# A feed-forward block's input products as 7 products in place of 8, in 2 x 2 blocks

## The chip, the cores and the metric

One Trainium2 chip; the program runs on one of its cores. The metric is the device time of one execution in microseconds (us). TensorE (PE) multiplies, VectorE (DVE), ScalarE (ACT) and GpSimd (POOL) work on tiles in SBUF and PSUM, SyncE (SP) issues the transfers from HBM.

## What is computed

One layer of a streaming encoder over 560 tokens (16 meta tokens, 512 frames of a new stream, 32 of a running one): a feed-forward block with its norm, a mixer (retention and latent attention), a norm, and a second feed-forward block with a norm. All in float32. The part that matters here:

```python
def swiglu(x, w_in, w_out):
    g, u = jnp.split(x @ w_in, 2, axis=-1)          # w_in 1024 x 5632
    return (jax.nn.silu(g) * u) @ w_out             # w_out 2816 x 1024

def ffn_block(x, w_in, w_out, g, b):
    return layer_norm(DN_ALPHA * x + 0.5 * swiglu(x, w_in, w_out), g, b)
...
h = ffn_block(h, ffn1_w_in, ffn1_w_out, ln1_g, ln1_b)
mix = jnp.concatenate([ret_y, mla_y], -1) @ w_mix_out
h = layer_norm(DN_ALPHA * h + mix, ln2_g, ln2_b)
return ffn_block(h, ffn2_w_in, ffn2_w_out, ln3_g, ln3_b)
```

## The kernel before

Activations lie with features on partitions: `xs[hf][k]` is row tile k (128 of the 1024 features) of token half hf, as a pair of a rounded part and the rest. Halves are 288 and 272 tokens in FFN 1 and the first norm, 272 and 272 from the mixer's output on, where the meta tokens are dropped. Products carry float32 in three matmuls (`mm3`): rounded weights by rounded and by remaining activations, remaining weights by rounded activations. Weights come from HBM in tiles of 128 x 1024 (`load_w`): ACT rounds one (`wh`, L155), DVE subtracts for the rest in two pieces of 512 (`wl`, L157).

A feed-forward block (`ffn`) takes 22 column pairs j, one tile of the gate's weights and one of the up weights. For each and for each half, 2 x 8 row tiles x 3 matmuls, then `glu`: ACT silu of the gate (L395), DVE times up (L396), ACT rounds `h` (L168), DVE takes the rest (L169). So a pair is 96 matmuls, and a block 2112 for its input products. The first two pairs are done row tile by row tile, half 0 and then half 1, since weights and inputs land then (FFN 1) or half 1 is still in its norm (FFN 2). After all pairs comes the output product over 22 inner tiles: row tiles m = 0 to 5 for both halves, then 6 and 7 of half 0, then 6 and 7 of half 1, so that half 0's norm runs beside half 1's products.

`LayerNorm` takes each finished row tile (`add`: residual from its pair in two DVE operations, L283 and L284, or an addition, L286), centres all 8 tiles when two are there (`centre`, L305, and `prep`, L275 and L276), sums up moments on POOL, the last on DVE (L319), and `finish` has PE sum them over the partitions, takes the root on DVE and scales.

The order on PE is what the class `Weave` emits: among tasks whose data should be there by an estimated clock, the one of highest priority goes on. On the other engines a scheduler sets the order, each engine goes through its list in turn, and an instruction that waits holds up those behind it. Pools limit what can be ahead: 3 raw weight tiles `wr`, 4 rounded `wh` and `wl`, 12 half tiles, 8 PSUM banks.

## Time and profile before

| | |
|---|---|
| runs | 1149.88, 1150.14, 1151.75 us (median 1150.14) |
| span of the profiled execution | 1151.2 us |
| PE busy | 1124.9 us, 98% |
| DVE, ACT, POOL busy | 558.9, 370.8, 150.6 us |
| PE's mean granted clock | 0.981 |

The times come from runs without the profiler, the rows of the trace from one profiled execution of 1151.2 us; its times are counted from the start of its span. FFN 1 fills about the first 400 us, the mixer the next 330, FFN 2 the rest.

### The profile page before, as it was taken

What the parts mean: (1) busy time and instruction counts of PE and PEld (TensorE: products, weight loads), DVE (VectorE), ACT (ScalarE), POOL (GpSimd) and SP (SyncE); (2) the same over time, 40 slices, a digit from 0 to 9 for tenths busy, and PEclk for the clock granted to TensorE, in tenths of its full rate; (3) what the DMA queues carried; (4) which work ended last, traced back from release to release, by engine and by line L of the source; (5) the groups of instructions that cost most, each with busy time, mean ns of one, the idle gap of its engine ahead of it and who ended that gap; (6) DMA issues with size and microseconds to landing.
All of it is one profiled execution on the core that took longest, in us unless ns stands there. A gap on an engine that the chain in (4) does not pass through costs nothing.

```text
span 1151.2 us, 20255 instructions
## 1 busy us (share of the span) xinstructions
PE 1124.9 (98%) x8505; PEld 1085.4 (94%) x8505; DVE 558.9 (49%) x1225; ACT 370.8 (32%) x709; POOL 150.6 (13%) x169
## 2 busy tenths in 40 slices
...
GB/s 235 100 102 74 83 101 74 83 96 74 87 88 88 137 181 70 30 91 42 38 42 38 60 115 23 53 96 89 89 95 75 95 90 82 94 83 88 83 133 78
DMA packets 34458, 99.90 MB, mean 87 GB/s; under 512 B 4352, under 2 KB 9856, under 8 KB 34368
## 3 DMA queue, kind: packets, MB, share of 16 engines
...
q14 instruction: 24, 0.20, 0.1%
...
## 4 chain that ended last, share of the span: by engine, by line
PE 87%; DVE 7%; issue 2%; ACT 2%; POOL 0%; DMA 0%; SPq 0%; DVEq 0%; POOLq 0%; ACTq 0%
PE ps L130 79%; PE sc L130 2%; PE ax L130 2%; DVE wl L157 1%; DVE y L366 1%; DVE lnd L319 1%; PE ro L130 1%; PE ex L130 1%; DMA w<-in_w1f 0%; ACT y L377 0%; DVE y L275 0%; PE sc L134 0%; PE kv L130 0%; ACT x L168 0%; DVE y L305 0%
## 5 line engine op out<-in xcount | busy, mean ns | idle before, releaser
L130 PE MATMUL ps<-x,wh 128*128 128x272 f32 (+1 forms) x3456 | 674.1, 293 | 0.8 <-POOL x L169 0.4
L130 PEld LDWEIGHTS ps<-x,wh 128*128 128x128 f32 x3456 | 553.0, 191 | 8.6 <-issue 4.9
L130 PE MATMUL ps<-x,wl 128*128 128x272 f32 (+1 forms) x1728 | 504.7, 292 | 0.0
L157 DVE TENSOR_TENSOR wl<-wr,wh 128x512 fp32r<-128x512 f32 (+1 forms) x340 | 237.8, 727 | 242.7 <-ACT wh L155 242.2
L130 PEld LDWEIGHTS ps<-x,wl 128*128 128x128 f32 x1728 | 329.9, 191 | 0.0
L155 ACT CAST wh<-wr 128x1024 fp32r<-128x1024 f32 (+1 forms) x170 | 173.4, 1021 | 345.1 <-PE ps L130 236.2
L130 PE MATMUL ps<-h,wh 128*128 128x272 f32 (+1 forms) x1408 | 269.7, 290 | 0.0
L130 PEld LDWEIGHTS ps<-h,wh 128*128 128x128 f32 x1408 | 222.3, 188 | 0.3
L130 PE MATMUL ps<-h,wl 128*128 128x272 f32 (+1 forms) x704 | 204.1, 290 | 0.0
L130 PEld LDWEIGHTS ps<-h,wl 128*128 128x128 f32 x704 | 132.6, 188 | 0.0
L396 DVE TENSOR_TENSOR sil<-sil,ps 128x272 f32<-128x272 f32 (+1 forms) x88 | 38.8, 441 | 181.1 <-PE ps L130 170.8
L319 POOL TENSOR_TENSOR lnd<-y,y 128x272 f32<-128x272 f32 (+1 forms) x4 | 11.3, 2820 | 592.1 <-DVE y L305 296.8
L168 ACT CAST h<-sil 128x272 fp32r<-128x272 f32 (+1 forms) x88 | 36.6, 419 | 129.9 <-DVE sil L396 129.9
L395 ACT ACTIVATE sil<-ps 128x272 f32<-128x272 f32 (+1 forms) x88 | 35.0, 397 | 78.3 <-PE ps L130 78.2
L169 DVE TENSOR_TENSOR h<-sil,h 128x272 fp32r<-128x272 f32 (+1 forms) x88 | 38.9, 443 | 21.9 <-ACT h L168 21.9
L312 ACT ACTIVATE y<-y 128x272 f32<-128x272 f32 (+1 forms) x48 | 20.0, 432 | 54.8 <-DVE y L286 43.8
L355 POOL TENSOR_TENSOR y<-y,lnmb 128x272 f32<-128x272 f32 (+1 forms) x30 | 26.3, 906 | 39.3 <-ACT lnmb L346 24.6
L319 POOL TENSOR_TENSOR lnd<-lnd,y 128x272 f32<-128x272 f32 (+1 forms) x20 | 18.7, 933 | 90.6 <-DVE y L286 90.5
L319 POOL TENSOR_TENSOR lnq<-lnq,y 128x272 f32<-128x272 f32 (+1 forms) x30 | 28.9, 964 | 8.6 <-ACT y L312 7.4
L467 DVE TENSOR_TENSOR rope<-ps,rt 64x272 f32<-64x272 f32 (+3 forms) x28 | 12.4, 444 | 29.8 <-PE ps L130 29.2
L130 PE MATMUL ps<-mix,wh 128*128 128x272 f32 x128 | 24.9, 291 | 0.0
L130 PE MATMUL ps<-mix,ww 128*128 128x272 f32 x192 | 24.4, 286 | 0.0
...
## 6 DMA issues: line engine op xcount, KB each, us to landing
wr<-in_w SPq DMA_DIRECT2D x84, 512.0 KB, 3.6
wr<-in_w1o SPq DMA_DIRECT2D x20, 512.0 KB, 3.5
wr<-in_wmix SPq DMA_DIRECT2D x20, 512.0 KB, 3.5
wr<-in_w2o SPq DMA_DIRECT2D x20, 512.0 KB, 3.5
wr<-in_wmo SPq DMA_DIRECT2D x8, 512.0 KB, 3.7
...
```

Of the source, the lines that this page charges most:

```text
L130: nc.tensor.matmul(out, lhsT, rhs, start=start, stop=stop)
L155: nc.scalar.copy(hi[:, :nb * P], raw[:, :nb * P])
L157: nc.vector.tensor_tensor(out=lo[:, c], in0=raw[:, c], in1=f32(hi[:, c]), op=ALU.subtract)
L168: nc.scalar.copy(x[:, 0, cs], src)
L169: (eng or nc.vector).tensor_tensor(out=x[:, 1, cs], in0=src, in1=f32(x[:, 0, cs]), op=ALU.subtract)
L312: nc.scalar.activation(self.lo(m), self.hi(m), AF.Square)
L319: e.tensor_tensor(out=acc, in0=part(0) if first else acc, in1=part(m), op=ALU.add)
L355: nc.gpsimd.tensor_tensor(out=self.hi(m), in0=self.hi(m), in1=mb, op=ALU.subtract)
L366: (nc.gpsimd if self.sink and self.wide and m > 5 else nc.vector).tensor_tensor(out=self.hi(m), in0=self.hi(m), in1=r, op=ALU.mult)
L395: nc.scalar.activation(s, pg[:, :n], AF.Silu)
L396: nc.vector.tensor_tensor(s, s, pu[:, :n], ALU.mult)
L467: nc.vector.tensor_tensor(t[lo_], src_ps[hi_], sin[hi_, cs], ALU.mult)
```

## The change

The input products of a column pair go by blocks: A is the pair's weights, gate and up by two halves of four row tiles (a11, a12 of the gate, a21, a22 of up), B the activations, the same halves of row tiles by two halves of tokens (b11, b21 of half 0, b12, b22 of half 1). Of Strassen's scheme in Winograd's form seven products of 4 row tiles are taken for eight: a11 b11, a12 b21, s2 t2, s1 t1, s3 t3, s4 b22, a22 t4. The sums s of weights are made for each pair by POOL (`quads`), the sums t of activations once for a block by DVE and POOL (`sums`), and the seven results are added up on DVE (`rest`). Pair 0 is done as before; pairs 1 and 2 take their first two products in half 0's part of the start (`early`). Token halves are equal now, 280 and 280 in FFN 1, by putting 8 of the 16 meta tokens at the end (`wrap` copies them back in the mixer). Low parts of `h` go from DVE to POOL. The residual is kept whole (`xr`). The output product comes in three parts, after 8, 8 and 6 pairs, each added into the residual; in the last, m = 0 and 1 go for both halves, then 2 to 7 of half 0, then of half 1. Weights are rounded in pieces of 512 on ACT too. The estimated time of a matmul in `Weave` is longer.

```diff
-NBIG = 63
+NBIG = 45
...
+NPART = 26
+NRAW = 4
...
 NA = 288
-NB = T - NA
+HB = T // 2
+HM = NM // 2
+TW = T + HM
 HQ = TQ // 2
+KQ = KD // 2
+NFIRST = 4
+GROUPS = (8, 8, 6)
 
...
-    def mm(out, lhsT, rhs, start, stop):
+    def mm(out, lhsT, rhs, start, stop, more=False):
         n = rhs.shape[-1]
-        nc.tensor.matmul(out, lhsT, rhs, start=start, stop=stop)
-        wv.t += max(25.0, n / 2.4 + 2.5) if rhs.dtype == F32R else max(58.0, n / 0.6 + 5.0)
+        nc.tensor.matmul(out, lhsT, rhs, start=start, stop=stop, skip_group_check=more)
+        wv.t += max(110.0, n / 2.4 + 11.7) if rhs.dtype == F32R else max(98.0, n / 0.6 + 8.0)
 
...
+    def load_raw(src, nb):
+        raw = wp.tile([P, 8 * P], F32, tag="wr", name=nm("wr"))
         nc.sync.dma_start(raw[:, :nb * P], src)
...
+        return raw
...
+    def rounded(src, n=4 * P, early=False):
+        hi, lo = [tp.tile([P, 2 * NA], F32R, tag="big", name=nm(s)) if early else part(F32R, s) for s in ("wh", "wl")]
+        nc.scalar.copy(hi[:, :n], src)
+        nc.vector.tensor_tensor(out=lo[:, :n], in0=src, in1=f32(hi[:, :n]), op=ALU.subtract)
+        return hi, lo
...
+    xr = [[xp_.tile([P, NA], F32, tag="xr", name=nm("xr")) for _ in range(KD)] for _ in range(2)]
...
     for k in range(KD):
...
-        tc.keep_in_program_order(nc.sync.dma_start(t, xa[k]))
+        tc.keep_in_program_order(nc.sync.dma_start(xr[0][k][:, :HB], xa[k]))
...
-        split(xs[0][k], slice(0, NA), t, nc.gpsimd if k % 2 else nc.vector)
-        nc.scalar.copy(first_h[q][:, c], raw)
-        nc.vector.tensor_tensor(first_l[q][:, c], raw, f32(first_h[q][:, c]), ALU.subtract)
+        split(xs[0][k], slice(0, HB), xr[0][k][:, :HB], nc.gpsimd if k % 2 else nc.vector)
+        first.append(rounded(raw, early=True))
...
-        t = half(s="xin")
-        last_in = tc.keep_in_program_order(nc.sync.dma_start(t[:, :NB], xb[k]))
+        last_in = tc.keep_in_program_order(nc.sync.dma_start(xr[1][k][:, :HB], xb[k]))
...
-        split(xs[1][k], slice(0, NB), t[:, :NB], nc.gpsimd)
+        split(xs[1][k], slice(0, HB), xr[1][k][:, :HB], nc.vector if k % 2 else nc.gpsimd)
...
+        def part(self, m, ps):
+            if self.scaled[m]:
+                nc.vector.tensor_tensor(self.hi(m), self.hi(m), ps[:, :self.n], ALU.add)
+            else:
+                nc.vector.scalar_tensor_tensor(self.hi(m), self.hi(m), self.scale, ps[:, :self.n], ALU.mult, ALU.add)
+            self.scaled[m] = True
...
-            if self.y[m] is None:
-                self.y[m] = tp.tile([P, 2, NA], F32, tag="big", name=nm("y"))
-                xh, xl = f32(self.xt[m][:, 0, self.cs]), f32(self.xt[m][:, 1, self.cs])
-                nc.vector.scalar_tensor_tensor(self.hi(m), xl, self.scale, ps[:, :n], ALU.mult, ALU.add)
-                nc.vector.scalar_tensor_tensor(self.hi(m), xh, self.scale, self.hi(m), ALU.mult, ALU.add)
-            else:
-                nc.vector.tensor_tensor(self.hi(m), self.hi(m), ps[:, :n], ALU.add)
+            self.part(m, ps)
...
             for m in range(8):
-                if self.y[m] is None:
-                    self.prep(m)
+                if self.scaled[m]:
+                    nc.vector.tensor_tensor(self.hi(m), self.hi(m), self.c, ALU.subtract)
                 else:
-                    nc.vector.tensor_tensor(self.hi(m), self.hi(m), self.c, ALU.subtract)
+                    nc.vector.scalar_tensor_tensor(self.hi(m), self.hi(m), self.scale, self.c, ALU.mult, ALU.subtract)
+                    self.scaled[m] = True
...
+    def quads(j, wi, e=(nc.gpsimd, nc.gpsimd)):
+        g, u = load_raw(wi(2 * j), KD), load_raw(wi(2 * j + 1), KD)
+        a11, a12, a21, a22 = g[:, :4 * P], g[:, 4 * P:], u[:, :4 * P], u[:, 4 * P:]
+        s1, s2, s4 = part(s="s1"), part(s="s2"), part(s="s4")
+        e[0].tensor_tensor(out=s1, in0=a21, in1=a22, op=ALU.add)
+        e[0].tensor_tensor(out=s2, in0=s1, in1=a11, op=ALU.subtract)
+        e[1].tensor_tensor(out=a21, in0=a11, in1=a21, op=ALU.subtract)
+        e[1].tensor_tensor(out=s4, in0=a12, in1=s2, op=ALU.subtract)
+        return a11, a12, {"s1": s1, "s2": s2, "s3": a21, "s4": s4, "a22": a22}
+    def ffn(first, wi, wo, cs, lns, ready=(None, None)):
+        n = cs[0].stop - cs[0].start
+        s_ = slice(0, n)
...
+        ts = {}
...
+        def sums():
+            for b in range(KQ):
+                b11, b21, b12, b22 = col(xr, b, 0), col(xr, b + KQ, 0), col(xr, b, 1), col(xr, b + KQ, 1)
+                t1, t2, t3, t4 = [half(n, "ts") for _ in range(4)]
+                for t, x, y, e in ((t1, b12, b11, nc.vector), (t2, b22, t1, nc.vector), (t3, b22, b12, nc.gpsimd),
+                                   (t4, b21, t2, nc.gpsimd)):
+                    e.tensor_tensor(out=t, in0=x, in1=y, op=ALU.subtract)
+                for name, t, e in (("t2", t2, nc.vector), ("t1", t1, nc.vector), ("t3", t3, nc.vector), ("t4", t4, nc.gpsimd)):
+                    ts[name, b] = pair("ts")
+                    split(ts[name, b], s_, t, e)
...
+        def product(ps, w, name, start=True):
+            for b in range(KQ):
+                c = slice(b * P, b * P + P)
+                mm3(ps[:, :n], lambda _: (w[0][:, c], w[1][:, c]), 0, right(name, b), s_, start and b == 0, b == KQ - 1, not start)
+        def keep(hf, j, sil, up):
+            nc.vector.tensor_tensor(sil, sil, up, ALU.mult)
             h[hf][j] = pair("h")
-            split(h[hf][j], slice(0, n), s)
...
+            split(h[hf][j], s_, sil, nc.gpsimd)
+        def silu(ps):
+            t = half(n, "sil")
+            nc.scalar.activation(t, ps, AF.Silu)
+            return t
+        def rest(j, t1, sil0, p2, f):
+            w = {i: rounded(f[i]) for i in ("s2", "s1", "s3", "s4")}
+            pb = bank()
+            product(pb, w["s2"], "t2")
+            nc.vector.tensor_tensor(t1, t1, pb[:, :n], ALU.add)
+            yield 0
+            pc = bank()
+            product(pc, w["s1"], "t1")
+            y5 = half(n, "y5")
+            nc.vector.tensor_tensor(y5, t1, pc[:, :n], ALU.add)
+            yield 0
+            pd = bank()
+            product(pd, w["s3"], "t3")
+            c22 = half(n, "c22")
+            nc.vector.tensor_tensor(c22, y5, pd[:, :n], ALU.add)
+            yield 0
+            pe = bank()
+            product(pe, w["s4"], "b22")
+            nc.vector.tensor_tensor(y5, y5, pe[:, :n], ALU.add)
+            nc.scalar.activation(y5, y5, AF.Silu)
+            keep(1, j, y5, c22)
+            yield 0
...
+            if sil0 is None:
+                sil0 = p2()
+                yield 0
+            product(pd, rounded(f["a22"]), "t4", False)
+            nc.vector.tensor_tensor(t1, t1, pd[:, :n], ALU.add)
+            keep(0, j, sil0, t1)
+            yield 0
...
+        def early():
...
+            for k in range(KD):
+                for u in range(4):
+                    w, b = first(k, u)
+                    mm3(ps[u][:, :n], w, b, xs[0][k], s_, k == 0, k == KD - 1 or u > 1 and k == KQ - 1, u > 1 and k >= KQ)
+                yield 0
+                if k == KQ - 1:
+                    for u in (2, 3):
+                        t1[u - 1] = big(NA, "t1")[:, :n]
+                        nc.scalar.copy(t1[u - 1], ps[u][:, :n])
+            sil0 = {u - 1: silu(ps[u][:, :n]) for u in (2, 3)}
+            sil = silu(ps[0][:, :n])
+            keep(0, 0, sil, ps[1][:, :n])
+            if ready[1]:
+                yield ready[1]
+            f = {1: quads(1, wi, (nc.gpsimd, nc.vector))[2]}
+            sums()
+            ps = [bank() for _ in range(2)]
+            for k in range(KD):
+                for u in range(2):
+                    w, b = first(k, u)
+                    mm3(ps[u][:, :n], w, b, xs[1][k], s_, k == 0, k == KD - 1)
+                yield 0
+            sil = silu(ps[0][:, :n])
+            keep(1, 0, sil, ps[1][:, :n])
+            f[2] = quads(2, wi, (nc.gpsimd, nc.vector))[2]
+            for j in (1, 2):
+                yield from rest(j, t1[j], sil0[j], None, f[j])
...
+        def column(j):
+            a11, a12, f = quads(j, wi)
+            pa = bank()
+            product(pa, rounded(a11), "b11")
+            t1 = half(n, "t1")
+            nc.scalar.copy(t1, pa[:, :n])
+            yield 0
+            w2 = rounded(a12)
+            def p2():
+                product(pa, w2, "b21", False)
+                return silu(pa[:, :n])
+            yield from rest(j, t1, None, p2, f)
...
+        def out(k0, nk, last):
+            def load(m):
+                return load_w(wo[m, :, k0 * P:(k0 + nk) * P], nk)
+            def products(ps, w, hf):
+                for k in range(nk):
+                    mm3(ps[:, :n], w, k, h[hf][k0 + k], s_, k == 0, k == nk - 1)
+                    if k % 4 == 3:
                         yield 0
...
+            add = (lambda l: l.add) if last else (lambda l: l.part)
+            for m in range(2 if last else 8):
+                w = load(m)
                 for hf in range(2):
...
+                    ps = bank()
+                    yield from products(ps, w, hf)
+                    add(lns[hf])(m, ps)
+            if last:
+                for hf in range(2):
+                    for m in range(2, 8):
+                        ps = bank()
+                        yield from products(ps, load(m), hf)
+                        lns[hf].add(m, ps)
+        yield from early()
+        j, k0 = 3, 0
+        for g, nk in enumerate(GROUPS):
+            while j < k0 + nk:
+                yield from column(j)
+                j += 1
+            yield from out(k0, nk, g == len(GROUPS) - 1)
+            k0 += nk
```

In all, PE has 7694 matmuls where it had 8198, DVE 1536 operations for 1228, ACT 1053 for 691, POOL 453 for 175, SP 239 transfers and others for 235.

**A column pair on DVE.** Before, from the product with `sil` of half 0 of one pair to that of the next: two products, the rest of `h`, four roundings.

```order
L396 TENSOR_TENSOR sil_102_775<-sil_102_775,ps_101_726 128x288
L169 TENSOR_TENSOR h_103_778<-sil_102_775,h_103_778 128x288
L157 TENSOR_TENSOR wl_124_966<-wr_122_963,wh_123_965 128x512 x2
L396 TENSOR_TENSOR sil_106_831<-sil_106_831,ps_105_782 128x272
L157 TENSOR_TENSOR wl_127_973<-wr_125_970,wh_126_972 128x512
L169 TENSOR_TENSOR h_107_834<-sil_106_831,h_107_834 128x272
```

Now, from the third addition of a pair (into `c22`) to the first of the next; `wl` of `s1`, `s2`, `s4` and of the raw tiles belong to the pair after the next.

```order
L465 TENSOR_TENSOR c22_173_813<-y5_171_798,ps_172_800 128x280
L159 TENSOR_TENSOR wl_217_1030<-wr_210_1017,wh_216_1029 128x512
L469 TENSOR_TENSOR y5_171_798<-y5_171_798,ps_174_815 128x280
L159 TENSOR_TENSOR wl_220_1048<-wr_210_1017,wh_219_1047 128x512
L159 TENSOR_TENSOR wl_222_1052<-s2_213_1022,wh_221_1051 128x512
L441 TENSOR_TENSOR y5_171_798<-y5_171_798,c22_173_813 128x280
L159 TENSOR_TENSOR wl_224_1056<-s1_212_1021,wh_223_1055 128x512
L477 TENSOR_TENSOR t1_158_749<-t1_158_749,ps_172_800 128x280
L159 TENSOR_TENSOR wl_226_1060<-wr_211_1019,wh_225_1059 128x512
L441 TENSOR_TENSOR sil_176_846<-sil_176_846,t1_158_749 128x280
L159 TENSOR_TENSOR wl_228_1064<-s4_214_1023,wh_227_1063 128x512
L159 TENSOR_TENSOR wl_238_1145<-wr_211_1019,wh_237_1144 128x512
```

The additions and the roundings take turns, seven roundings to a pair where four stood.

**A column pair on POOL**, which had nothing there before: the sums for the pair after the next, then the low parts of this pair's `h` of half 1 and half 0.

```order
L402 TENSOR_TENSOR s1_212_1021<-wr_211_1019 128x512
L403 TENSOR_TENSOR s2_213_1022<-s1_212_1021,wr_210_1017 128x512
L404 TENSOR_TENSOR wr_211_1019<-wr_210_1017,wr_211_1019 128x512
L405 TENSOR_TENSOR s4_214_1023<-wr_210_1017,s2_213_1022 128x512
L184 TENSOR_TENSOR h_175_831<-y5_171_798,h_175_831 128x280
L184 TENSOR_TENSOR h_179_866<-sil_176_846,h_179_866 128x280
```

The four sums stand ahead of the low parts.

**ACT at the start of FFN 1.** Before, the last casts of half 1's inputs (`x` from `xin`) stand behind the first silu.

```order
L168 CAST x_39_180<-xin_38_178 128x272
L395 ACT_TABLE_LOAD
L395 ACTIVATE sil_54_335<-ps_50_235 128x288
L168 CAST x_41_185<-xin_40_183 128x272
L395 ACTIVATE sil_56_341<-ps_52_237 128x288
L168 CAST x_43_190<-xin_42_188 128x272
```

Now all eight casts of half 1 stand ahead of the two copies of `t1` (the first products of pairs 1 and 2, whose PSUM banks go on to take the second ones) and of the silu.

```order
L183 CAST x_54_207<-xr_13_91 128x280
L183 CAST x_55_211<-xr_14_92 128x280
L183 CAST x_56_215<-xr_15_93 128x280
L183 CAST x_57_219<-xr_16_94 128x280
L495 COPY t1_62_301<-ps_60_251 128x280
L495 COPY t1_63_303<-ps_61_252 128x280
L447 ACT_TABLE_LOAD
L447 ACTIVATE sil_64_353<-ps_60_251 128x280
```

The copies came to the head of the silu and behind the last input.

## Rows read from the trace of the kernel before

**Rows 1.** The page, parts 1 and 4: busy times; the chain that ended last

```profile
PE 1124.9 (98%) x8505; PEld 1085.4 (94%) x8505; DVE 558.9 (49%) x1225; ACT 370.8 (32%) x709; POOL 150.6 (13%) x169
...
PE ps L130 79%; PE sc L130 2%; PE ax L130 2%; DVE wl L157 1%; DVE y L366 1%; DVE lnd L319 1%; PE ro L130 1%; PE ex L130 1%; DMA w<-in_w1f 0%; ACT y L377 0%; DVE y L275 0%; PE sc L134 0%; PE kv L130 0%; ACT x L168 0%; DVE y L305 0%
```

**Rows 2.** Timeline of PE in FFN 1 and 2: start, us, engine, line, operation

```profile
108.18 0.29 PE L130 MATMUL ps<-x,wl 128*128 128x288 f32 x1
...
108.98 0.29 PE L130 MATMUL ps<-x,wl 128*128 128x288 f32 x1
...
799.81 0.29 PE L130 MATMUL ps<-x,wl 128*128 128x272 f32 x1
...
800.93 0.29 PE L130 MATMUL ps<-x,wl 128*128 128x272 f32 x1
```

**Rows 3.** Windows, FFN 2: busy PE, PEld, DVE, ACT, POOL, clock, DMA, GB/s

```profile
775.00:800.00 25.00, 25.00 (x202) 25.00 (x201) 8.89 (x17) 7.23 (x13) 0.00 (x0) 1.00 0.27 86
```

**Rows 4.** Groups by form on DVE: busy us, mean ns of one, idle before

```profile
L157 DVE TENSOR_TENSOR wl<-wr,wh 128x512 fp32r<-128x512 f32 x296 | 213.0, 745 | 181.7 <-ACT wh L155 181.3
L396 DVE TENSOR_TENSOR sil<-sil,ps 128x272 f32<-128x272 f32 x66 | 28.9, 437 | 102.0 <-PE ps L130 99.6 <-ACT sil L395 2.2
```

**Rows 5.** Groups by form on POOL: the operation on 512 columns

```profile
L779 POOL TENSOR_TENSOR q<-q,qd 128x512 f32<-128x512 f32 x4 | 5.1, 1277 | 38.6 <-PE rsc L130 23.6 <-issue 15.0
```

**Rows 6.** Timeline of DVE in FFN 2, while POOL rests

```profile
785.76 0.69 DVE L157 TENSOR_TENSOR wl<-wr,wh 128x512 fp32r<-128x512 f32 x1 [0.50 <-ACT wh L155]
786.37 0.43 DVE L169 TENSOR_TENSOR h<-sil,h 128x272 fp32r<-128x272 f32 x1
786.72 0.68 DVE L157 TENSOR_TENSOR wl<-wr,wh 128x512 fp32r<-128x512 f32 x1
```

**Rows 7.** Timelines of DVE and of POOL at the same time, third norm

```profile
1124.13 1.01 DVE L365 TENSOR_TENSOR y<-y,lnmb 128x272 f32<-128x272 f32 x1
1125.06 1.01 DVE L227 TENSOR_TENSOR lnt<-lnt 128x272 f32<-128x272 f32 x1
...
1122.35 4.36 POOL L355 TENSOR_TENSOR y<-y,lnmb 128x272 f32<-128x272 f32 x5 [10.41 <-ACT lnmb L334]
```

**Rows 8.** Timelines of the start: SP's issues, ACT, PE

```profile
10.02 3.89 SPq L196 DMA_DIRECT2D xin<-in_xb  x8
...
17.56 1.38 SPq L140 DMA_DIRECT2D wr<-in_w  x3
...
13.60 1.39 ACT L168 CAST x<-xin 128x288 fp32r<-128x288 f32 x4
...
18.96 0.42 PE L130 MATMUL ps<-x,wh 128*128 128x272 f32 x2
```

**Rows 9.** DMA issues of the start: KB each, median us to landing

```profile
xin<-in_xb SPq DMA_DIRECT2D x8, 136.0 KB, 3.5
...
wr<-in_w SPq DMA_DIRECT2D x6, 512.0 KB, 4.1
```

**Rows 10.** Windows of 4 us at the first norm, columns as in rows 3

```profile
424.00:428.00 4.00, 1.45 (x12) 1.25 (x10) 3.76 (x9) 0.00 (x0) 2.95 (x5) 0.93 0.83 284
428.00:432.00 4.00, 4.00 (x16) 3.77 (x17) 3.52 (x11) 2.27 (x6) 0.45 (x1) 0.50 0.01 4
432.00:436.00 4.00, 4.00 (x26) 4.00 (x26) 3.70 (x9) 4.00 (x10) 1.86 (x3) 0.72 0.00 0
```

**Rows 11.** Timeline of DVE: the last split of half 1 ahead of FFN 2

```profile
751.09 0.44 DVE L169 TENSOR_TENSOR x<-y,x 128x272 fp32r<-128x272 f32 x1 [1.21 <-ACT x L168]
```

**Rows 12.** Timelines of DVE and of POOL while FFN 2's tiles are centred

```profile
1046.95 0.78 DVE L276 SCALAR_TENSOR_TENSOR y<-x,y 128x272 f32<-128x272 f32 x2
...
1046.40 4.78 POOL L319 TENSOR_TENSOR lnd<-y,y 128x272 f32<-128x272 f32 x1 [4.25 <-DVE y L305]
```

**Rows 13.** Timeline of DVE: half 0's and half 1's last add in FFN 2

```profile
1117.71 0.44 DVE L286 TENSOR_TENSOR y<-y,ps 128x272 f32<-128x272 f32 x1 [0.46 <-PE ps L130]
...
1136.15 0.43 DVE L286 TENSOR_TENSOR y<-y,ps 128x272 f32<-128x272 f32 x1
```

211 lines of the change are left out of this document (83 added, 128 removed).

## Prediction

> **What bounds the kernel now.** I read the page's busy shares first, then its chain of waits, then the timeline of the feed-forward blocks. TensorE (PE) is busy 98% of the span and makes 87% of the chain, 79% in products into `ps` [rows 1]. In a stretch of FFN 2 PE is busy all 25 of 25 us at full clock while VectorE (DVE) has 8.9, ScalarE (ACT) 7.2 and GpSimd (POOL) nothing [rows 3]. So a product taken away there is time taken away, until another engine becomes late. What a product costs is its distance to the next: nine of 272 columns pass between 799.81 and 800.93, 124.4 ns each; six of 288 between 108.18 and 108.98, 133.3 ns [rows 2]. For 280 columns I take the middle, 128.9 ns, which is also the mean that FFN 1 pays now for its halves of 288 and 272.
>
> **What the change removes.** Each of 21 column pairs takes 7 products of 4 row tiles by 3 matmuls, 84, where it took 96; the order has 504 matmuls less (8198 to 7694). FFN 1: 252 x 128.9 ns = 32.5 us; FFN 2: 252 x 124.4 ns = 31.4 us. Together **-63.9 us**, all on the path. A column now lasts 10.8 us (FFN 1) or 10.45 (FFN 2) on PE, 10.65 in the mean.
>
> **What a column adds.** On DVE 5 operations with one operand in PSUM (437 ns, the product with `sil` [rows 4]), two of 272 to 280 columns with both inputs in SBUF, and 7 roundings of 512. With POOL idle DVE starts the next operation 0.61 us after a rounding and 0.35 us after a two-input operation of 272 [rows 6]: 5 x 0.44 + 2 x 0.35 + 7 x 0.61 = 7.2 us. On POOL four sums of 512, for which the nearest row is 1277 ns [rows 5], and two low parts of `h` at 0.87 (4.36 us for five [rows 7]): 6.9 us. Each fits in 10.65 alone. Together they don't run side by side: beside POOL's five, DVE's two-input operations came 0.93 us apart (1124.13, 1125.06 [rows 7]), so that a POOL operation of 272 took 0.58 us from DVE; for one of 512 I scale by length, 1.09. If half to two thirds of POOL's operations meet a two-input operation of DVE, as its 5.0 us of those in 10.65 suggest, DVE needs 7.2 + 0.5 to 0.65 x (4 x 1.09 + 2 x 0.58) = 10.0 to 10.8 us: just what PE takes. Weights are rounded a column ahead and the wait that binds, the last product's for the addition that gave `c22`, has some 3 us of slack, so I take **+2 us** in all (0 to 6). By the order 22 columns of the 38 that are built this way are so loaded: the last two or three of a group have output weights to round, for which POOL does nothing, and the sums of a group's first columns stand beside the output product before it.
>
> The pair of operations in [rows 7] cost 0.93 us where 0.35 + 0.87 would be 1.22: the two engines hinder each other, but not for an operation's whole length. The Trainium skill's page "SBUF — State Buffer", section "Who interferes with whom", says more: a DVE instruction with two SBUF inputs and a GpSimd one that reads SBUF shut each other out for the whole instruction. By that rule the steady term would be 25 us more than the 2 taken here, and the time that of rival (c); the trace bears it out only in part.
>
> **FFN 1's start.** PE's first half, 96 products of 288, is over at 18.96 [rows 8], so it ran as if without gaps from 6.2. Now the third matmul group of row tile 4 needs ACT's copy of `t1`, which stands behind all eight casts of `xs[1]`. Those inputs are issued from 10.02 to 13.9 [rows 8]; the last of them lands 3.5 us after [rows 9], at some 17.2, and a cast and a copy (four casts take 1.39 [rows 8]) give 18.0. PE is there after 54 products, 6.2 + 7.0 = 13.1: **+4.9 us** (4 to 6). It then has 90 products, to 29.6, and 9 of the next product, 1.2 us, until it needs the last low part of `t2`. The raw weights that POOL and DVE add up first are issued from 17.56 [rows 8] and land after 4.1 [rows 9], the first pair at 22.3. From there DVE has 28 rows to that low part: 9 of 512, 18 of 280, one of PSUM, alone 9 x 0.61 + 18 x 0.36 + 0.44 = 12.4 us (at 34.7); with POOL's 4 sums and 10 shorter operations all in the way, + 4 x 1.09 + 10 x 0.58 = 22.6 us (44.9). The middle is 39.8, half a microsecond more for the waits on POOL's `s2`: **+9.5 us** (4 to 14). After such idle time the clock falls: in 424 to 428 PE worked 1.45 of 4 us, and the granted clock then was 0.50 (1.2 GHz) and 0.72 [rows 10], (0.07 + 0.50 + 0.28) x 4 = 3.4 us lost. I count one such fall here: **+3.4 us** (0 to 7).
>
> **FFN 2's start.** The last split of `xs[1]` is over at 751.5 [rows 11]; PE has from there 57 products, to 758.6. DVE has 27 rows to the last low part of `t2`: 8 x 0.61 + 18 x 0.35 + 0.44 = 11.6 us alone, 4 x 1.09 + 13 x 0.58 = 11.9 more with POOL in the way: 763 to 775, a wait of 4 to 16. I take **+9 us** and one fall of the clock, **+3.4 us** (0 to 7).
>
> **The groups' ends.** Each output product's first half needs the low part of the last column's `h`: 0.44 + 0.35 + 0.35 + 0.87 us over DVE, DVE, ACT and POOL, a rounding of 0.61 between, 2.6 us and the handovers; PE has 21 products, 2.6 us, until then. 0 to 1 us, six times: **+3 us**. In the last group half 0's six adds now follow each other every 18 products, 13.4 us in all, and beside them DVE has both halves' centring, 16 x 0.35, six tiles' roundings, 6 x (0.61 + 0.33), and 7 adds, 14.3 us alone, with POOL's moments (up to 14 x 0.58 = 8) in the way; so the last add comes 1 to 9 us late, and PE waits for its moments. And only 108 products of half 1 lie over half 0's norm, where 132 did, 3.0 us less; at the end of the kernel that norm's DVE work already filled 18.4 us from half 0's last add to half 1's (1117.71, 1136.15 [rows 13]), more than the products. **+9 us** for both blocks (4 to 18).
>
> **The rest.** The residual is kept whole, so an add is one operation instead of two, and the mixer's work is set by slightly later estimates of time. In between lie -3 and +4 us, **+1**. SP's four more transfers and the casts in pieces of 512 are off the path: DMA is at 0.27 and ACT busy 7.2 of 25 us now [rows 3], and if that cover went, PE would wait for `wh`.
>
> **Sum.** -63.9 + 2 + 4.9 + 9.5 + 3.4 + 9 + 3.4 + 3 + 9 + 1 = **-18.7 us**. The profiled execution has a span of 1151.2, and the runs' median is 1150.1, 1.1 less: 1132.5 for a profiled span, **1131** for the median. With the terms between their bounds, which won't all lie at one end, 1116 to 1147.
>
> **Rivals.**
> (a) *The sums hide.* If DVE and POOL meet seldom, both starts go at the price alone (4 us each), the clock doesn't fall, the group ends cost nothing and the norms 4: -63.9 + 4.9 + 4 + 4 + 4 = -47, about **1103**. For it: DVE and POOL are nearly free now [rows 3]. Against it: in the starts both have their longest unbroken queues of two-input operations, and PE nothing else to do.
> (b) *DVE and POOL bound the loaded columns; slower than before.* If every POOL operation meets one of DVE's, a loaded column takes 7.2 + 5.5 = 12.7 us, 2.05 more than PE: 22 x 2.05 = 45, less the 2 counted, **1174**. Where POOL gets the worst of it, it may be later still: beside an unbroken row of DVE's a single operation of 272 took 4.78 us [rows 12]. It decides from a loaded column of 11.65 us upwards: there 22 x 1.0 eats what is left. For it: the free time counted above is next to nothing. Against it: DVE's operations on PSUM and its waits leave POOL gaps that [rows 7 and 12] don't have.
> (c) *They shut each other out for whole operations.* Then DVE's two-input work and POOL's can't overlap at all, but DVE's PSUM operations run beside POOL: 5.0 + 6.9 = 11.9 us a loaded column, 22 x 1.25 = 27.5, less 2: **1156**, a little slower than before. That is the rule of the page named above. Against it: 0.93 for 1.22.
>
> That the products are not left out at all can't be, by the count of the order.
>
> **Chances.** The forecast 0.55, (a) 0.20, (b) 0.15, (c) 0.10. Of the last two together, with columns between 11.4 and 13 us, 0.15 ends slower, 0.05 within 0.2% (2.3 us, about what a measurement can tell from no change) and 0.05 still faster. So faster 0.80, same 0.05, slower 0.15. The range that leaves out 0.08 below and 0.12 above: 1102 to 1156.
>
> **What would show it.** In the profile after: PE idle from about 13 to 18 us and from 31 to 40, and about 759 to 768 later by what was gained, each with a clock of 0.5 behind it; columns of 10.8 and 10.5 us with PE without idle time (forecast, (a)) or of over 11.6 with PE waiting for `wl` or `ps` freed by DVE (b); POOL's sums of 512 near 1.3 us, or over 2; a wait of some microseconds behind half 0's last add in both norms. Wrong above all would be a column that DVE sets, or a second wait of FFN 1 that ends before 35 us.

## The result, and the profile after

The changed kernel takes **1180.45 us** (median of 4 runs, 1176.0 to 1181.25), the kernel before 1150.82 beside it (1149.88 to 1151.75): 1.0246 times as long, 95% interval 1.0225 to 1.0267. It is slower by 2.5%, where the prediction said 1131 and at most 1156.

Busy times and the chain that ended last, from the page of the changed kernel, as in [rows 1]:

```profile
PE 1093.7 (93%) x8001; PEld 1044.3 (89%) x8001; DVE 802.9 (68%) x1533; ACT 486.1 (41%) x1071; POOL 482.4 (41%) x447
...
PE ps L143 67%; DVE wl L159 3%; PE sc L143 2%; DVE xr L307 2%; PE ax L143 2%; DVE ts L184 1%; DVE lnd L325 1%; ACT wh L158 1%; DVE ts L425 1%; DVE xr L283 1%; DMA xr<-in_xa 1%; PE lnst L143 1%; DVE xr L372 1%; PE ro L143 1%; PE ex L143 1%
```

PE is busy 93% where it was 98; products into `ps` make 67% of the chain where they made 79. Windows of the two feed-forward blocks' inner columns, with [rows 3] (busy PE, PEld, DVE, ACT, POOL, then clock, DMA share, GB/s):

```profile
200.00:225.00 25.00, 25.00 (x195) 24.90 (x194) 21.77 (x31) 12.77 (x27) 18.20 (x15) 1.00 0.26 85
...
925.00:950.00 25.00, 25.00 (x201) 25.00 (x200) 22.38 (x35) 14.14 (x31) 16.94 (x13) 1.00 0.34 106
```

In these two windows PE still has no idle time, with DVE busy 22 of 25 us and POOL 17 to 18. From one column to the next 84 products take 10.83 us in FFN 1, as worked out, but for seven columns, the first three and three in the second group among them, that take 10.96 to 11.59. In FFN 2 they take 10.45 us before the first output product, as worked out, and 10.58 behind it, at granted clock 1.00 in both. So the columns give most of the 63.9 us back, and the loss is elsewhere: in the starts of both blocks and at their ends. The starts in windows of 12 us, same columns:

```profile
28.00:40.00 12.00, 5.03 (x26) 3.72 (x24) 11.51 (x16) 5.62 (x15) 9.14 (x9) 0.77 0.20 70
40.00:52.00 12.00, 7.64 (x31) 6.87 (x31) 10.89 (x17) 6.41 (x15) 8.18 (x8) 0.52 0.14 44
52.00:64.00 12.00, 9.35 (x73) 9.12 (x71) 11.44 (x15) 4.93 (x10) 8.62 (x8) 1.00 0.29 89
...
782.00:794.00 12.00, 3.12 (x8) 1.87 (x8) 11.87 (x15) 3.38 (x9) 10.21 (x10) 0.64 0.15 44
794.00:806.00 12.00, 10.08 (x56) 9.54 (x55) 8.82 (x17) 5.53 (x12) 3.93 (x6) 0.65 0.14 44
```

Before, PE is busy 12.00 of 12 us at clock 1.00 in each of the first three. Now it is busy 5 and 8, and in the second works at half clock: 31 products where 12 us hold 95. Meanwhile DVE is busy 11 to 12 of 12, in all five windows but the last.

What PE waits for there (longest first: us in total, times, longest), 10 to 70 us and then 745 to 800:

```profile
PE ps L143 <- DVE wl L159: 4.9, 1, 4.9
PE ps L143 <- DVE c L465: 3.7, 1, 3.7
PE ps L143 <- ACT t L495: 3.6, 1, 3.6
PE ps L143 <- DVE ts L184: 3.1, 2, 2.0
PE ps L143 <- ACT ts L183: 2.6, 2, 1.3
...
PE ps L143 <- ACT ts L183: 6.8, 3, 3.2
PE ps L143 <- ACT t L495: 5.3, 1, 5.3
PE ps L143 <- DVE ts L184: 4.9, 3, 2.8
```

`ts` are the sums of activations, `t` (L495) the copies of the first products, `c` (L465) the addition into `c22`.

At the blocks' ends, the waits of the whole span that belong to the norms:

```profile
PE lnst L143 <- DVE lnd L325: 16.5, 5, 7.1
...
PE lnr L143 <- DVE lndg L253: 9.2, 4, 2.5
...
PE lnmu L143 <- DVE lnd L325: 7.1, 1, 7.1
```

Two waits of 7.1 us stand out, one in each block: PE wants half 0's sums of moments. DVE at that place in FFN 1 (start, us, line, operation), to set beside [rows 12 and 13]:

```profile
398.56 5.93 DVE L307 TENSOR_TENSOR xr<-xr,lnc 128x280 f32<-128x280 f32 x8
404.41 0.79 DVE L283 TENSOR_TENSOR xr<-xr,ps 128x280 f32<-128x280 f32 x2
...
408.00 0.43 DVE L283 TENSOR_TENSOR xr<-xr,ps 128x280 f32<-128x280 f32 x1
```

Half 1's centring (L307, eight tiles, 5.93 us) stands between half 0's adds. Half 0's last product is over at 401.1, its last add begins at 408.0, 6.9 us later. Twelve of half 1's 108 products still run until 402.6; the other 96 stand in PE's order behind the product that waits for the moments, so they can't cover the wait.

**The account**, from PE's marks in both profiled executions (us over the kernel before at the same place):

| term | predicted | measured |
|---|---|---|
| products left out | -63.9 | -63.9 |
| columns and groups' ends | +5 | +7.2 |
| FFN 1's start | +17.8 | +27.4 |
| FFN 2's start | +12.4 | +24.5 |
| ends of both blocks and their norms | +9 | +28.4 |
| mixer and second norm | +1 | +4.6 |
| sum | -18.7 | +28.2 (the spans: +28.2) |

A start's figure is the time to the first product of column 3 less its products at 128.9 or 124.4 ns and less what was lost over as many products before: in FFN 1 67.80 - 6.15 - 264 x 0.1289 = 27.6, of which 0.2 was lost before; in FFN 2 813.78 - 747.54 - 264 x 0.1244 = 33.4, of which 8.9 was lost before. An end's is worked out in the same way, from the first product of the last output product to the mixer's first moments or the end of the span: 15.6 us in FFN 1 and 12.8 in FFN 2.

### The profile page after: what moved, and what is told of

Same layout as the page of the kernel before. It is cut to its first block, busy times and chain, and to the rows that moved or that the text cites. A ratio compares the mean times of both kernels' runs of the same rounds, so it can differ in the third digit from the quotient of the medians.

```text
span 1179.3 us, 20644 instructions
## 1 busy us (share of the span) xinstructions
PE 1093.7 (93%) x8001; PEld 1044.3 (89%) x8001; DVE 802.9 (68%) x1533; ACT 486.1 (41%) x1071; POOL 482.4 (41%) x447
## 4 chain that ended last, share of the span: by engine, by line
PE 77%; DVE 13%; issue 4%; ACT 3%; POOL 2%; DMA 1%; SPq 0%; DVEq 0%; POOLq 0%; ACTq 0%
PE ps L143 67%; DVE wl L159 3%; PE sc L143 2%; DVE xr L307 2%; PE ax L143 2%; DVE ts L184 1%; DVE lnd L325 1%; ACT wh L158 1%; DVE ts L425 1%; DVE xr L283 1%; DMA xr<-in_xa 1%; PE lnst L143 1%; DVE xr L372 1%; PE ro L143 1%; PE ex L143 1%
## 5 line engine op out<-in xcount | busy, mean ns | idle before, releaser
L143 PE MATMUL ps<-x,wh 128*128 128x272 f32 (+1 forms) x1776 | 359.9, 299 | 8.9 <-ACT t L495 8.9
L159 DVE TENSOR_TENSOR wl<-wr,wh 128x512 fp32r<-128x512 f32 x348 | 288.4, 834 | 106.2 <-ACT wh L158 62.6
L143 PEld LDWEIGHTS ps<-x,wh 128*128 128x128 f32 x1776 | 288.5, 194 | 15.8 <-ACT t L495 9.4
L158 ACT CAST wh<-wr 128x512 fp32r<-128x512 f32 x348 | 204.1, 601 | 237.6 <-PE ps L143 219.8
L143 PE MATMUL ps<-ts,wh 128*128 128x280 f32 (+1 forms) x1344 | 270.7, 297 | 23.0 <-ACT ts L183 9.4
L143 PE MATMUL ps<-h,wh 128*128 128x280 f32 (+1 forms) x1408 | 275.5, 293 | 2.3 <-POOL h L184 1.8
L143 PE MATMUL ps<-x,wl 128*128 128x272 f32 (+1 forms) x888 | 261.3, 294 | 0.0
L143 PEld LDWEIGHTS ps<-ts,wh 128*128 128x128 f32 x1344 | 217.0, 193 | 28.6 <-ACT ts L183 11.0
L143 PE MATMUL ps<-h,wl 128*128 128x280 f32 (+1 forms) x704 | 204.6, 291 | 0.0
L143 PE MATMUL ps<-ts,wl 128*128 128x280 f32 (+1 forms) x672 | 197.4, 294 | 4.9 <-DVE wl L159 4.9
```

Source lines behind the costliest of these rows:

```text
L143: nc.tensor.matmul(out, lhsT, rhs, start=start, stop=stop, skip_group_check=more)
L158: nc.scalar.copy(hi[:, :n], src)
L159: nc.vector.tensor_tensor(out=lo[:, :n], in0=src, in1=f32(hi[:, :n]), op=ALU.subtract)
```

## Experiments

Stages below are cut at PE's marks in each run's profile: **start** (beginning of the block to its first output product), **columns** (from there to the first matmul of the last of the three output products), **end** (from there to the mixer, or the end of the span). So the first five columns lie in the start. The changed kernel has 123.7, 252.6, 92.9 us in FFN 1 and 118.5, 245.8, 67.5 in FFN 2. One thing must be known to read the medians: the mixer, which no edit touches, takes 215.7 to 220.0 us in the profiled executions, 220.0 in the changed kernel's, since the granted clock falls there for longer in some than in others. Two windows of the same work, the changed kernel's and the first experiment's:

```profile
500.00:530.00 30.00, 30.00 (x177) 24.88 (x176) 12.45 (x34) 13.03 (x31) 4.37 (x4) 0.77 0.27 88
```

```profile
485.00:515.00 30.00, 30.00 (x198) 25.57 (x197) 14.61 (x39) 14.59 (x36) 4.41 (x4) 0.89 0.30 96
```

So differences of up to 4 us in the medians are read from the stages alone. The columns of FFN 2, too, came out 1.5 us shorter in two runs whose edits touch nothing there.

### Which sums: of activations, or of weights

The sums of activations left out; products take the input tiles in their place.

```diff
             if name[0] == "t":
-                return ts[name, b]
+                return xs[1 if name in ("t1", "t2") else 0][b if name in ("t1", "t3") else b + KQ]
...
-            sums()
```

> Leaves out the sums of activations of both feed-forward blocks (16 subtractions, 16 splits each): the products take tiles of the inputs in their place, so the output is another. Theory S (the time lies in the two starts, where TensorE waits for these sums, made by VectorE and GpSimd in turns, and then runs at 1.2 GHz): the starts, which lose 27 and 25 us more than before, keep some 8 and 9 (the copies of t1, the weights' landing), so about 1180 - 35 = 1145 us. Rival K (the loaded columns cost the time, the starts little): no more than 5 us less, 1175 us.

Measured: 1146.36 us, 0.9957 of the kernel before (0.9943 to 0.9972). The starts are 15.0 and 14.0 us shorter, the mixer 4.3. The window of the start, 28 to 53 us, of the changed kernel and then of this one:

```profile
28.00:53.00 25.00, 13.67 (x64) 11.59 (x63) 23.40 (x34) 12.03 (x29) 18.32 (x17) 0.66 0.17 55
```

```profile
28.00:53.00 25.00, 22.21 (x159) 21.81 (x158) 23.77 (x34) 12.02 (x24) 16.71 (x12) 0.93 0.33 112
```

PE is busy 22.2 us for 13.7, at clock 0.93 for 0.66. What the sums are made with costs 29 us, all in the starts; the other 5 of the median's 34 are the mixer's and the second norm's, which no edit touched. Of the 52 us that the starts lost, 23 are left without the sums.

The sums of weights left out from the fourth column on, where the columns' work is loaded most.

```diff
     def quads(j, wi, e=(nc.gpsimd, nc.gpsimd)):
         g, u = load_raw(wi(2 * j), KD), load_raw(wi(2 * j + 1), KD)
         a11, a12, a21, a22 = g[:, :4 * P], g[:, 4 * P:], u[:, :4 * P], u[:, 4 * P:]
+        if j > 2:
+            return a11, a12, {"s1": a21, "s2": a11, "s3": a21, "s4": a12, "a22": a22}
```

> Leaves out the four sums of weights of column pairs 3 to 21 in both blocks (152 GpSimd operations on 512 columns): the products take the raw pieces, rounded as the sums were. Theory S: the columns lose only 3.7 and 4.0 us to groups' ends and all, so at most 8 us less there and 4 in the second pair of the start, 1168 to 1180 us. Rival K: the loaded columns lose over 0.5 us each, 20 us or more come back, 1160 us or less.

Measured: 1167.24 us, 1.014 (1.0113 to 1.0168). The columns gain 1.1 and 1.3 us, although POOL loses most of its work there (FFN 2 in its windows):

```profile
925.00:950.00 25.00, 25.00 (x201) 25.00 (x201) 18.49 (x35) 13.84 (x28) 3.73 (x4) 1.00 0.33 102
```

POOL 3.73 for 16.94, DVE 18.5 for 22.4, and PE the same 25.00. So rival (b) of the prediction, that DVE and POOL bound the columns, is out, and (c) with it. Of the two gains only FFN 1's 1.1 can be put down to the sums (all its columns take 10.83 us now), since FFN 2's columns vary by as much without an edit. The run gains 8.4 us in FFN 1's start, where the sums of the next columns fall into the same stretch: the wait for `c22` at 61 to 65 us (3.7) and the clock's fall behind it don't occur, and the first three columns take 10.83 us each where they took 11.59, 11.42 and 11.19. The mixer gives 4.3 by itself.

### The starts

Pairs 0 and 1 as before the change (both halves, 96 products each), the sums made beside half 1.

```diff
-                    mm3(ps[u][:, :n], w, b, xs[0][k], s_, k == 0, k == KD - 1 or u > 1 and k == KQ - 1, u > 1 and k >= KQ)
...
-            sums()
...
-            for j in (1, 2):
-                yield from rest(j, t1[j], sil0[j], None, f[j])
+            for hf in range(2):
+                if hf:
+                    sums()
+                ps = [bank() for _ in range(4)]
+                for k in range(KD):
+                    for u in range(4):
+                        w, b = first(k, u)
+                        mm3(ps[u][:, :n], w, b, xs[hf][k], s_, k == 0, k == KD - 1)
...
-        j, k0 = 3, 0
+        j, k0 = 2, 0
```

> Pairs 0 and 1 the old way, row tile by row tile, seven products from pair 2 on: 24 more matmuls (3 us), but 96 products of half 1 instead of 48 stand over the sums of activations, and no copy of t1 is needed there. Theory S: the starts' loss falls from 27 and 25 us to under 8 each, 1180 - 36 + 3 = 1147 us. Rival M (the work on VectorE and GpSimd takes as long and TensorE only waits later): less than 10 us gained, 1170 us or more.

Measured: 1154.31 us, 1.0032 (1.0015 to 1.005), starts 7.3 and 11.4 us shorter though each has 12 products more (1.5 us). By the stages that is 18.7 us, where the first expectation had 33 and the second under 10: between the two. The mixer and the second norm, 5.4 us, bring the median nearer to the first than that. The longest wait left from 10 to 72 us:

```profile
PE ps L143 <- ACT wh L158: 6.3, 1, 6.3
```

It is for column 2's rounded weights, which ACT casts and DVE splits behind all the sums. So the wait has moved, from the sums to what stands behind them.

The copies of the first products made on DVE in place of ACT, where they stood behind eight casts.

```diff
-                        nc.scalar.copy(t1[u - 1], ps[u][:, :n])
+                        nc.vector.tensor_copy(t1[u - 1], ps[u][:, :n])
```

> The copies of t1 in the starts are made by VectorE instead of ScalarE, so that they don't stand behind ScalarE's casts of half 1's inputs. Theory: the first waits of the two starts (3.6 us at 13 us and 5.3 us at 762 us, each followed by 1.2 GHz) go, but the second waits end when the sums are made, as before, so FFN 1 gains nothing and FFN 2 at most 5: 1175 to 1180 us. Rival (what goes first is gained): 9 us or more less, 1171 us.

Measured: 1180.07 us, 1.0245 (1.0212 to 1.0277). Nothing is gained, but the waits for the copies didn't go: in FFN 1 the 3.6 us become 4.6, for DVE, and in FFN 2 the 5.3 become two of 3.9 and 0.6, with a wait of 2.7 ahead of them grown to 5.4. So what it would be worth to be rid of them, no run shows.

The same sums in another order: t1 and t2 of all four row tiles and the low parts of t2, which the first waiting product needs, ahead of the others.

```diff
+            for b in range(KQ):
...
+                nc.vector.tensor_tensor(out=d["t1", b], in0=col(xr, b, 1), in1=col(xr, b, 0), op=ALU.subtract)
+                nc.vector.tensor_tensor(out=d["t2", b], in0=col(xr, b + KQ, 1), in1=d["t1", b], op=ALU.subtract)
+                low(b, "t2", nc.vector)
+            for b in range(KQ):
+                low(b, "t1", nc.vector)
+            for b in range(KQ):
...
+                nc.gpsimd.tensor_tensor(out=d["t3", b], in0=col(xr, b + KQ, 1), in1=col(xr, b, 1), op=ALU.subtract)
+                nc.gpsimd.tensor_tensor(out=d["t4", b], in0=col(xr, b + KQ, 0), in1=d["t2", b], op=ALU.subtract)
+                low(b, "t3", nc.vector)
+                low(b, "t4", nc.gpsimd)
```

> The changed kernel with the sums of activations made in another order: t1 and t2 of all four row tiles and the low parts of t2 first, then the low parts of t1, then t3 and t4. Same operations on the same engines. Theory W (the work sets the wait: until all sums are made PE gets no second product): the last low part of t2 comes some 7 us earlier (39 instead of 46 us), PE makes its 9 products of s2 t2 that waited (1.2 us, 2.4 at 1.2 GHz), and then waits for the rounding of s1, which stands on DVE behind all low parts, to about 45. Gain 2 to 4 us per block, 1173 to 1178 us. Rival O (the order was the fault: the part needed first was made last): both starts lose 6 to 8 us each less, 1165 to 1169 us.

Measured: 1175.78 us, 1.0204 (1.0168 to 1.0241); starts 0.7 and 1.7 us shorter, the mixer 3.0. PE's products at the ends of two of the waits there (the bracket: idle time and what ended it):

```profile
36.07 0.60 PE L143 MATMUL ps<-ts,wl 128*128 128x280 f32 x1 [1.33 <-DVE wl L159]
44.70 0.83 PE L143 MATMUL ps<-ts,wh 128*128 128x280 f32 x2 [5.93 <-ACT wh L158]
```

The product with t2 is made 8 us earlier, and the next one waits to 44.70 for the rounding of s1, which stands on ACT behind the casts of all sums. POOL had made s1 at 22.8; ACT came to cast it at 44.0:

```profile
21.48 1.28 POOL L402 TENSOR_TENSOR s<-wr 128x512 f32<-128x512 f32 x1 [2.81 <-DMA wr<-in_w]
```

```profile
44.04 0.61 ACT L158 CAST wh<-s 128x512 fp32r<-128x512 f32 x1
```

From 37.6 to 44.0 ACT rests 4.1 us, waiting for POOL's sums. So to have t2 first isn't enough while another operand of the next product stands behind all sums. That the order is without weight isn't shown: an order with the casts of s1, s3 and s4 ahead wasn't tried.

All sums of activations made on DVE, which has twelve operations more, and POOL none.

```diff
-                for t, x, y, e in ((t1, b12, b11, nc.vector), (t2, b22, t1, nc.vector), (t3, b22, b12, nc.gpsimd),
-                                   (t4, b21, t2, nc.gpsimd)):
+                for t, x, y, e in ((t1, b12, b11, nc.vector), (t2, b22, t1, nc.vector), (t3, b22, b12, nc.vector),
+                                   (t4, b21, t2, nc.vector)):
...
-                for name, t, e in (("t2", t2, nc.vector), ("t1", t1, nc.vector), ("t3", t3, nc.vector), ("t4", t4, nc.gpsimd)):
+                for name, t, e in (("t2", t2, nc.vector), ("t1", t1, nc.vector), ("t3", t3, nc.vector), ("t4", t4, nc.vector)):
```

> The changed kernel with all sums of activations and their low parts on VectorE; GpSimd keeps the weights' sums and the low parts of h. Theory T (VectorE and GpSimd take turns on operations that read two tiles of SBUF): VectorE does 12 operations more, 4.3 us alone, but 12 of GpSimd's no longer hold it up, 12 x 0.58 = 7 us, so the second waits end some 3 us earlier in each start: 1174 us. Rival (the two engines work side by side): 4 us later in each start, 1188 us.

Measured: 1172.59 us, 1.019 (1.0163 to 1.0217); starts 4.6 and 1.1 us shorter, the mixer 4.3. DVE has more to do and is done sooner. Its timeline in the changed kernel, with POOL's two operations beside it, and then here, where POOL rests from 28.9 to 42.0:

```profile
34.73 1.02 DVE L425 TENSOR_TENSOR ts<-xr,xr 128x280 f32<-128x280 f32 x1
...
36.27 2.32 DVE L184 TENSOR_TENSOR ts<-ts,ts 128x280 fp32r<-128x280 f32 x3
38.52 0.43 DVE L425 TENSOR_TENSOR ts<-xr,ts 128x280 f32<-128x280 f32 x1
...
35.98 1.01 POOL L184 TENSOR_TENSOR ts<-ts,ts 128x280 fp32r<-128x280 f32 x1 [0.54 <-ACT ts L183]
36.95 0.98 POOL L425 TENSOR_TENSOR ts<-xr,xr 128x280 f32<-128x280 f32 x1
```

```profile
32.65 1.52 DVE L184 TENSOR_TENSOR ts<-ts,ts 128x280 fp32r<-128x280 f32 x4
34.09 0.43 DVE L425 TENSOR_TENSOR ts<-xr,xr 128x280 f32<-128x280 f32 x1
```

Three splits took 2.25 us to the next operation beside POOL, four take 1.44 alone: 0.75 and 0.36 each, so two POOL operations of 280 took 1.17 us from DVE, 0.58 each, the price that the prediction had from [rows 7]. The whole stretch agrees: from 24.6 to 45.9 us DVE had 27 operations, 11.8 us alone by the prediction's prices, and POOL twelve short ones and two of 512, 9.1 us by its price of a meeting; 21.3 us passed. So nearly every one was in the way.

Dummy products (28 in each start) between the waiting ones, so that PE isn't idle.

```diff
+                if fill:
+                    spare = bank("fill")
+                    for _ in range(fill):
+                        nc.tensor.matmul(spare[:, :P], warm, warm, start=True, stop=True)
...
-            product(pb, w["s2"], "t2")
+            product(pb, w["s2"], "t2", True, 7 if j == 1 else 0)
```

> 28 products of zeros, some 0.4 us each, into a bank that nobody reads, stand in TensorE's wait for the sums of activations in each start, 7 ahead of each row tile of pair 1's first product, so that TensorE has some 12 us of work in it; nothing else is changed. Theory C (the idle time is followed by 1.2 GHz, and the products behind the wait lose by that): the clock stays at 2.4 GHz behind both waits, the 24 to 36 products there go at 0.13 instead of 0.25 us, 5 to 6 us less, 1175 us. Rival: the sums set the time until later than that, under 2 us less or more than before.

Measured: 1173.61 us, 1.0201 (1.0167 to 1.0235). Starts 2.6 and 1.1 us shorter, the mixer 4.3, the second norm 1.3. In 28 to 53 us the clock is 0.86 where it was 0.66:

```profile
28.00:53.00 25.00, 16.32 (x106) 15.46 (x104) 25.00 (x35) 12.74 (x29) 18.56 (x17) 0.86 0.14 44
```

The median falls as expected, but more than half of it is the mixer's and the norm's, so the run supports the theory on the clock by the granted clock and by 3.7 us alone. Once PE runs at full clock it waits again for DVE: the rounding of 4.9 us is still there.

### The ends

Half 0's and half 1's centring begun after the second group's first two row tiles, an output product before the last.

```diff
+                self.begin()
+
+        def begin(self):
+                n = self.n
...
                     add(lns[hf])(m, ps)
+                    if mid and m == 1:
+                        lns[hf].begin()
```

> The centring of the feed-forward blocks' norms is begun after the second group's output product (the mean of its first two row tiles) instead of in the last group. Theory E (the two ends lose 16 and 13 us more than before, since 16 centring operations stand between the last group's adds on VectorE): 14 to 18 us less, about 1164 us. Rival L (the last group's short products, 108 over half 0's norm where 132 stood, are what it costs): under 6 us less, 1175 us or more.

Measured: 1163.61 us, 1.0109 (1.0077 to 1.0142); the ends are 7.7 and 7.8 us shorter. DVE's last add of half 0 in FFN 1, and PE's wait for the moments from 388 to 440 us:

```profile
400.79 0.45 DVE L283 TENSOR_TENSOR xr<-xr,ps 128x280 f32<-128x280 f32 x1
```

```profile
PE lnst L143 <- DVE lnq L329: 2.6, 1, 2.6
PE lnst L143 <- DVE lnd L329: 1.9, 2, 1.7
```

The add comes 7.2 us earlier, as half 0's products end (400.8), and the wait of 7.1 us is gone. In FFN 2 the first wait of 7.1 is gone too, but the one for half 1's moments grows from 4.2 to 7.0.

Groups of 6, 8 and 8 pairs, so that the last group's half 1 has 144 products over half 0's norm where it had 108.

```diff
-GROUPS = (8, 8, 6)
+GROUPS = (6, 8, 8)
```

> The groups are 6, 8 and 8 pairs instead of 8, 8 and 6: the last output product's row tiles take 24 matmuls instead of 18, so the adds are 3.1 us apart instead of 2.3, and 144 products lie over half 0's norm where 108 did. Theory E (the centring between those adds is what costs at the ends): VectorE's queue has 0.8 us more for each of 12 row tiles, up to 4 us less at each end, 1172 to 1176 us. Rival L (the cover over half 0's norm alone): 4.6 us less at both ends, 1171 us; under 2 us: neither.

Measured: 1162.63 us, 1.0096 (1.0074 to 1.0118). Both expectations were some 10 us too high: with the two more pairs' 96 output products taken off, the ends are 8.4 and 6.3 us shorter, the mixer 4.3. PE's waits for the norms fall to 5.0 (`lnst`) and 4.5 (`lnmu`) from 7.1 each. I had put two effects against each other as rivals: half 0's adds come further apart, 24 products for 18 (up to 4 us at each end), and the cover is longer (36 products, 4.6 us at each end). The 14.7 us are more than either gives and less than both; the run doesn't part them.

### Together

Pairs 0 to 2 as before the change, with pair 2's weights rounded ahead of the sums, and the early centring. The additions to the edits above:

```diff
+                    ws = [load_w(wi(4 + i), KD) for i in range(2)]
...
+            for hf in range(2):
+                ps = [bank() for _ in range(2)]
+                for u in range(2):
+                    for k in range(KD):
+                        mm3(ps[u][:, :n], ws[u], k, xs[hf][k], s_, k == 0, k == KD - 1)
...
+                keep(hf, 2, silu(ps[0][:, :n]), ps[1][:, :n])
```

> Pairs 0 to 2 the old way, with the third pair's weights rounded ahead of the sums of activations, and the centring begun after the second group, as in the run that did that alone: 24 more matmuls (3 us) than the changed kernel. Theory S and E together: the starts, which lose 27 and 25 us more than before, keep under 5 each, 42 us less, and the ends give the 17 us that the centring gave alone: 1180 - 59 + 3 = 1124 us. Rival M (the sums' work then holds up the first columns instead): 1140 us or more.

Measured: 1131.65 us, 0.9825 (0.9801 to 0.9849). It is faster than the kernel before, 7.7 us slower than expected. Three of these are a slip in the expectation: it has 24 matmuls more in each block, 48 in all, 6 us and not 3. And the sums are late even now (waits 40 to 60 us, FFN 1):

```profile
PE ps L143 <- DVE ts L184: 3.6, 2, 2.5
PE ps L143 <- ACT ts L183: 3.4, 1, 3.4
```

The same with groups of 6, 8 and 8:

> The run with three old-way pairs and the early centring, with groups of 6, 8 and 8 pairs. Theory E says that cover and queue at the ends are two sides of one wait: with the centring gone from the last group the larger group gives only the part that cover is, 36 products over half 0's norm, 2 to 4 us at each end: 1125 us. If the larger group's 18 us were a gain of its own, 1114 us; if they were the centring's, 1131 us.

Measured: 1122.56 us, 0.976 (0.9736 to 0.9784), another 9 us. With the early centring and the larger last group together the ends are 13.7 and 12.7 us shorter than the changed kernel's, 26.4 of the 28.4 that they had lost.

And with the sums of activations on DVE:

> Both of the others of this call together. By theory T another 2 to 6 us less than the first of them, 1120 us; by its rival as much more, 1130 us.

Measured: **1117.15 us**, 0.9709 (0.9687 to 0.973), 2.9% less than the kernel before. Its start of FFN 1 and what PE waits for from 10 to 72 us:

```profile
28.00:53.00 25.00, 25.00 (x196) 25.00 (x195) 22.45 (x48) 13.53 (x34) 9.16 (x8) 1.00 0.15 47
```

```profile
PE ps L143 <- DVE c L469: 5.0, 1, 5.0
```

DVE makes the same sums, and PE works beside them without a pause at full clock.

## Why the prediction was wrong

**Right: what is taken out, and the columns.** 504 products are 63.9 us at the prices read before. The loaded column stayed PE's, at 10.83 us in FFN 1 but for a few, and 10.45 or 10.58 in FFN 2; columns and groups' ends cost 7.2 us for 5: 2.8 in seven columns of FFN 1, 2.3 in waits for `h` at the groups' ends, and the rest by the products' slower pace in FFN 2. DVE was busy 22.4 of 25 us there, 9.5 of 10.65, a little under the 10.0 to 10.8 worked out; without nine of POOL's sums its 35 operations took 18.5. POOL's sums took longer than the 1277 ns of [rows 5], and DVE's roundings longer than the 745 of [rows 4]:

```profile
L159 DVE TENSOR_TENSOR wl<-wr,wh 128x512 fp32r<-128x512 f32 x318 | 273.7, 865 | 96.3 <-ACT wh L158 52.8 <-PE ps L143 37.3 <-issue 0.4
...
L402 POOL TENSOR_TENSOR s<-wr 128x512 f32<-128x512 f32 x42 | 62.3, 1483 | 166.7 <-PE ps L143 159.6
...
L405 POOL TENSOR_TENSOR s<-wr,s 128x512 f32<-128x512 f32 x38 | 62.2, 1638 | 3.0 <-PE ps L143 3.0
```

yet the columns kept PE's pace but for those few. Rival (b) gave 1174, near the time measured, by a mechanism that the second experiment shows is not there; that nearness means nothing. (c) falls by the same run.

**Wrong: FFN 1's start, 27.4 for 17.8.** The first wait is there (3.6 us for 4.9, by L495). The second was to end at 34.7 to 44.9, taken in the middle, 39.8; the last low part of t2 came at 45.9. The price of a meeting was right (0.58 us, shown above); the step that failed is the middle between "alone" and "all in the way". In a start both engines have an unbroken queue, and the nearest row, [rows 7], was one where every operation meets: the upper end was the value to take. The prediction said as much of the starts in its case against rival (a), and didn't use it in the sum. A further wait, for `c22` at 61 to 65 us (3.7), wasn't priced at all; it comes from the sums of the next columns' weights, since it is gone where these are left out. And the clock: PE's idle time grew by 18.1 us in the windows from 6 to 76 us, so some 9 of the 27.4 were, by subtraction, products at half clock, where one fall of 3.4 stood in the sum. The clock was 0.50 for all of 36 to 44 us:

```profile
36.00:40.00 4.00, 2.15 (x5) 1.29 (x5) 4.00 (x7) 1.90 (x5) 2.90 (x3) 0.50 0.33 120
40.00:44.00 4.00, 0.96 (x3) 0.50 (x2) 4.00 (x7) 1.83 (x5) 2.36 (x4) 0.50 0.00 0
```

since the wait was not one but five, with a few products between them. I had counted one wait and one fall.

**Wrong: FFN 2's start, 24.5 for 12.4.** The same copy of t1 on ACT holds PE here too, 5.3 us (L495); it was priced for FFN 1 and forgotten here, a plain omission. The waits for `ts` come to 11.7 us where 9 stood, and the clock again for longer than one fall: 0.64 and 0.65 in 782 to 806. How much of the loss is the omission's isn't shown: the run with the copies on DVE left most of that wait in place.

**Wrong most of all: the ends, 28.4 for 9.** The lateness of half 0's last add was in the range (6.9 us, "1 to 9"), and it is the wait of 7.1, in each block. The step that failed is the size: 9 us for both blocks, 4.5 each, are less than that one wait, and the term held no fall of the clock. Behind the first late moments PE waits four times more in FFN 1 (2.0, 0.9, 2.9 and 2.5 us; `lndg`, `lnd`, `lnq`), where it waited 1.2 and 2.6 before, with 3.0 us less of products over the norm's steps, and the clock falls to 0.77 and 0.80 in 400 to 424:

```profile
400.00:412.00 12.00, 4.86 (x38) 4.66 (x37) 10.91 (x18) 4.32 (x13) 6.63 (x8) 0.77 0.32 96
412.00:424.00 12.00, 9.98 (x56) 9.40 (x56) 10.09 (x27) 5.97 (x14) 10.40 (x8) 0.80 0.63 191
```

Beginning the centring earlier takes 15.5 us of the 28.4, a larger last group 14.7 (each alone), both together 26.4, so the causes shown are the centring in DVE's queue and the short last group, its cover and the spacing of its adds in one.

**The rest, 4.6 for 1**, is mixer and second norm; since the mixer varies by 4.3 from one execution to another, no cause is to be named.

**The turn-taking rule.** The Trainium skill's page "SBUF — State Buffer", section "Who interferes with whom", has a DVE instruction with two SBUF inputs and a GpSimd one that reads SBUF shut each other out for the whole instruction. Here a POOL operation of 280 columns took 0.58 us from DVE. What it takes by itself the prediction had wrong: the 0.87 us of [rows 7] were measured beside DVE and hold POOL's own waiting. While DVE rests (39.3 to 40.5 us in the run with t2 first) they follow each other every 0.73 us:

```profile
39.26 0.77 POOL L434 TENSOR_TENSOR ts<-xr,xr 128x280 f32<-128x280 f32 x1
39.99 0.78 POOL L435 TENSOR_TENSOR ts<-xr,ts 128x280 f32<-128x280 f32 x1
```

So a meeting costs DVE about four fifths of the operation: less than the whole, but nearer to it than the prediction's 0.93 for 1.22 made it look. In the loaded columns, for which rival (c) worked out 11.9 us, PE kept 10.83 in FFN 1 and 10.45 to 10.58 in FFN 2.

**What stays open.** How much of the ends' 28.4 is the clock and how much the norm's chain itself wasn't separated by a run; by PE's idle time, which grew by 22.7 us there, some 6 are left for the clock. To put half 0's moments further back in PE's order, so that more of half 1's 96 products cover the wait, wasn't tried either. Of the 23 us that the starts still lose without the sums of activations, the trace of that run names the copies' waits (3.3 and 5.3 us), those for `c22` (3.8 and 1.0) and the clock, but no run takes all of them away. Of the version at 1117.15 the gain is 34 us where its products alone (57.8: 63.9 less 48 products at 127 ns) would give more. By the account used above its starts still lose 7.6 and 6.5 us, its columns and groups' ends 8.3, the ends of the blocks only 1.2 more than before. So what is left lies ahead of the ends: the largest wait that its profile names there is for `c22` (9.6 us), and what would take it away wasn't tried.
